# First shift and scale of an adaLN block: float32 weights straight to TensorE, in 32-column tiles of the array

## The chip, the cores and the metric

The kernel runs as one program on one NeuronCore of a Trainium2 chip. The metric is the device time of one execution in microseconds, and the median of three executions of the kernel before is 2047.05 us (2043.01 to 2047.86). The profile is of one further execution. PE is TensorE, DVE is VectorE, ACT is ScalarE, POOL is GpSimd and SP is SyncE, which issues the loads of the weights.

## The reference

One layer of a backbone is applied to 128 context tokens and 128 latent tokens, in float32, with a model width D of 2048. All of it lies behind a modulation that is computed from two conditioning vectors, `c_ctx` for the context tokens and `c` for the latent ones:

```python
mod = silu(c) @ w_mod + b_mod                       # w_mod is 2048 x 12288
shift1, scale1, gate1, shift2, scale2, gate2 = split(mod, 6)
h  = rmsnorm(x, norm1_g) * (1 + scale1) + shift1
...                                                 # w_in, three mixer branches, merge
x  = x + gate1 * (merged @ w_out)
h2 = rmsnorm(x, norm2_g) * (1 + scale2) + shift2
x  = x + gate2 * (square(relu(h2 @ w_ff1)) @ w_ff2)
```

So `w_mod` has six parts of 2048 x 2048. Of each part, two rows are wanted: one for each conditioning vector.

## The kernel before

**Units.** All weights come in units of 128 x 1024 float32 (512 KB). `run_stream` (L390) walks one list of steps for the whole layer. A step that holds a unit is prefetched: SP loads it into one of eight raw buffers (L399), and `split` (L384) turns it into two float32r tiles, a rounded one on ACT (`wh`) and the rest on DVE (`wl`). There are five buffers for such pairs (L400). PE multiplies each pair in three products per tile: high by high, low by high, high by low. This is the code of almost every group on the page, and it all carries line 171, that of the helper which records each call, so that groups are told apart by the names of the tiles.

**The first two parts of `w_mod`** (shift1 and scale1) are 64 units, `in_wmods`, in eight blocks of 256 columns. They go through the same split. For each k-tile, `do` (L656) multiplies the 128 x 512 high tile by a stationary tile of four columns (the high and low parts of silu(c) and silu(c_ctx)), and the 128 x 512 low tile by its first two columns. The result is a 4 x 512 row block in PSUM. After a block, `chain` (L678) copies the block out, turns it by four small matmuls with the constant `sel`, adds the bias, and makes the 256 rows of the modulated, normalised input `Hh`, `Hl` that go with these columns. The first 24 units of the input projection `w_in` (`in_win`, `in_winh`) stand between the 64 units, one after every two or three of them, from the 14th on.

**The other four parts** (gate1, shift2, scale2, gate2) take another way: `mods` (L732) is a background generator. It loads `in_wmodr` units by SP into three buffers `mraw`, and DVE multiplies each unit by a broadcast vector `cb` and sums it: two instructions per unit, one for each vector, into `junk` and `part`. That is 128 units and 256 such instructions. Each part has two halves of 16 units. Between halves the one `cb` buffer is loaded anew by POOL, and an add moves `part` into `modc`.

**What sets their order.** Nothing but the planner in the kernel does: `pump` (L302) lets generators go on while its model of the clock says that DVE and ACT are not behind PE. `mods` also waits for a quota (L757): unit m may be taken once `self.units`, which counts the steps that `run_stream` has done (L445), has reached `quota(m)` (L723). The quota is drawn through five marks (L1440, L1532, L1708), which are counts of all units in the list of steps. At three places the rest is forced, whatever the quota says. Part 2 is wanted by the output projection. Parts 3 and 4 are wanted ahead of the last piece of the output projection, in `drain_mod` (L1593, L1805), since the second norm needs them. Part 5 is wanted in `gates2` (L1679), which stands between the two halves of the third group of the second MLP matrix; there `chunk_rows` (L1733) turns the vector by a PE transpose and sends it to memory.

Of the kernel before, what the change touches and what calls it, by code (L numbers as in the profile page):

```python
# [7 lines left out]
F32 = mybir.dt.float32  # L8
# [6 lines left out]
P = 128  # L15
# [101 lines left out]
class Meter:  # L117
# [5 lines left out]
    def cost(self, name, a, k, out):  # L123
        n = int(np.prod(out.shape[1:]))
        src = k.get("in0", k.get("in_", a[1] if len(a) > 1 else out))
        ps = getattr(src, "space", None) == bass.MemoryType.PSUM
        if self.key == "pe":
            if name == "transpose":
                return max(n * 8.5e-4, 0.107)
            return n * 4.17e-4 + 0.0133 if k["rhs"].dtype == F32R else max(n * 1.7e-3, 0.22)  # L130
        if self.key == "act":
            fn = a[2] if len(a) > 2 else None
            extra = 0.0
            if fn in TABLES and self.clock.table != fn:
                self.clock.table, extra = fn, 1.3
            extra += 0.093 * sum(isinstance(k.get(x), bass.AP) for x in ("scale", "bias", "accum_out"))
            return (0.053 if ps else 0.095) + n * 8.3e-4 + extra
        if self.key == "pool":
            return 0.1 + n * 1.0e-3
        if name == "tensor_reduce":  # L140
            n = int(np.prod(src.shape[1:]))
        one = name in ("tensor_scalar", "tensor_copy", "memset") and not ps
        c = 0.07 + n * (6.3e-3 if name == "reciprocal" else 5.2e-4 if one else 1.04e-3)
        if isinstance(k.get("scalar", k.get("scalar1")), bass.AP):
            c += 0.06
        if "accum_out" in k:
            c += 0.116
        return c
# [46 lines left out]
class Backbone:  # L195
# [194 lines left out]
    def run_stream(self, steps):  # L390


        nc = self.nc
        units = [s["unit"] for s in steps if "unit" in s]
        raw, hl = [], {}
        st = dict(dma=0, front=0)
        t = self.t

        raws = [None] * 3 + [3, 4, 5, 6, 7]  # L399
        pairs = [None] * 3 + [8, 9]  # L400

        def issue():
            while raws and st["dma"] < len(units):
                n = st["dma"]
                z = raws.pop(0)
                u = units[n]
                if z is None:
                    w = self.rawp.tile([P, NB], F32, tag="raw", name=self.nm("raw"))[:, :u.shape[1]]
                else:
                    w = self.slot(z, [P, NB])  # L410
                nc.sync.dma_start(w, u)
                raw.append((w, self.clock.dma + DMA1, z))
                st["dma"] += 1

        def front():
            n = st["front"]
            s = steps[n]
            st["front"] += 1
            if "unit" not in s:
                return  # L420
            w, at, z = raw.pop(0)
            c = w.shape[1]
            p = pairs.pop(0)
            if p is None:
                hi = self.hlp.tile([P, NB], F32R, tag="wh", name=self.nm("wh"))[:, :c]
                lo = self.hlp.tile([P, NB], F32R, tag="wl", name=self.nm("wl"))[:, :c]
            else:
                both = self.slot(p, [P, 2, NB], F32R)
                hi, lo = both[:, 0, :], both[:, 1, :]
            self.split(hi, lo, w)  # L430
            hl[n] = (hi, lo, p, max(t["act"], t["dve"]) + READY)
            if z is None or st["dma"] < self.lend - 8:
                raws.append(z)
            issue()

        issue()
        for i, s in enumerate(steps):
            while st["front"] < len(steps) and pairs and not ("hold" in s and st["front"] > i):
                if st["front"] > i and raw and raw[0][1] > t["pe"] + 1.5:
                    break  # L440
                front()
            if s["kind"] == "mm":
                hi, lo, p, _ = hl.pop(i)
                s["do"](hi, lo)
                self.units += 1  # L445
                self.next = min((v[3] for v in hl.values()), default=0.0)
                self.pump()
                self.next = 0.0
                if p is None or st["dma"] < self.lend:
                    pairs.append(p)  # L450
            elif s["kind"] == "call":
                s["do"]()
# [49 lines left out]
    def setup(self):  # L502
        nc, I = self.nc, self.I
        c = lambda name, shape, dt=F32: self.cp.tile(shape, dt, tag=name, name=name)
        self.xin = [self.slot(10, [P, 8, 256]), self.slot(11, [P, 8, 256])]
        j, cv = self.take()
        cv = cv[:, :32]
        nc.sync.dma_start(cv, I["cvec"])
        for i in range(2):
            nc.sync.dma_start(self.xin[i], I["xT"][:, 8 * i:8 * i + 8, :])  # L510
        self.modc = c("modc", [P, 6, 16, 2])
        self.gs = c("gs", [P, 2, 16, 2])
        self.sel = c("sel", [4, 2])
        nc.scalar_dma.dma_start(self.sel, I["sel"])

        self.cs = c("cs", [P, 16, 2])
        nc.scalar.activation(self.cs.rearrange("p k v -> p (k v)"), cv, AF.Silu)
        self.puttmp(j)
        self.cst = c("cst", [P, 16, 4], F32R)
        self.split(self.cst[:, :, 0:2], self.cst[:, :, 2:4], self.cs)  # L520
        self.par = c("par", [P, 386])
        nc.scalar_dma.dma_start(self.par, I["par"])
        self.ident = c("ident", [P, P])
        nc.scalar_dma.dma_start(self.ident, I["ident"])
        self.tri = c("tri", [P, 4, P])
        self.hmask = c("hmask", [P, 7, P], U8)
        self.rows = c("rows", [P, 32])
        par = self.par
        self.bmod = par[:, 0:96].rearrange("p (c n) -> p c n", c=6)
        self.n1g, self.n2g = par[:, 96:112], par[:, 112:128]  # L530
        self.hlb = par[:, 128:144]
        self.hgn, self.gdnn = par[:, 144:145], par[:, 145:146]
        self.vng = par[:, 146:154]
        self.conv = par[:, 154:370].rearrange("p (n w) -> p n w", n=24)
        self.ones = c("ones", [P, P])
        nc.vector.memset(self.ones, 1.0)
        self.lb = c("lb", [P, 16])
        self.junk = c("junk", [P, 1024], mybir.dt.bfloat16)
        self.junk2 = c("junk2", [P, 512], mybir.dt.bfloat16)
        self.oml = c("oml", [P, 16])  # L540
# [82 lines left out]
    def start_steps(self, first, second):  # L623
# [32 lines left out]
        def do(db, u, hi, lo):  # L656
            if u == 0:
                if db >= 2:
                    self.finish(self.chains[db - 2])
                st[db] = self.grab()  # L660
            if (db, u) == (4, 0):
                self.hm = self.mid(2, [P, 7, P])
                nc.gpsimd.dma_start(self.hm, self.I["hmask"])
                nc.gpsimd.dma_start(self.tri, self.I["tri"])
                nc.gpsimd.dma_start(self.rows, self.I["rows"].partition_broadcast(P))
            if (db, u) == (6, 0):
                self.add(bounds())
                self.spread()
            o = st[db][1]
            for j in range(2):  # L670
                k = 2 * u + j
                w = slice(512 * j, 512 * j + 512)
                nc.tensor.matmul(o[:4], lhsT=self.cst[:, k, :], rhs=hi[:, w], start=(k == 0), stop=False, skip_group_check=True)
                nc.tensor.matmul(o[:2], lhsT=self.cst[:, k, 0:2], rhs=lo[:, w], start=False, stop=(k == 15), skip_group_check=True)
            if u == 7:
                self.chains[db] = self.add(chain(db), first=True)

        def chain(db):  # L678
            i, b = st[db]
            row = self.mid(db % 2, [P, 512])  # L680
            nc.scalar.copy(row[:4], b[:4])
            yield W
            for t in range(4):
                nc.tensor.matmul(b[:, 2 * t:2 * t + 2], lhsT=row[:4, t * P:t * P + P], rhs=self.sel, start=True, stop=True)
            yield W
            n0 = 2 * db
            nc.vector.tensor_tensor(out=self.modc[:, 0:2, n0:n0 + 2, :],
# [4 lines left out]
            while "r" not in st:  # L692
# [1 line left out]
            yield from self.modulate(0, n0, self.xin[n0 // 8][:, n0 % 8:n0 % 8 + 2, :], st["r"])  # L694

        steps = []
        mods = [[dict(kind="mm", unit=self.I["wmods"][db, u], do=lambda hi, lo, db=db, u=u: do(db, u, hi, lo))
                 for u in range(8)] for db in range(8)]
        wins = []
        for db in range(8):  # L700
# [1127 lines left out]
def layout(x_prompt, x_sample, c, state_hgrn, state_gdn, c_ctx, norm1_g, norm2_g, w_mod, b_mod, w_in,  # L1828
# [21 lines left out]
        m = 1 << j  # L1850
        hm[:, j] = (i[:, None] // (2 * m) == i[None] // (2 * m)) & (i[:, None] // m != i[None] // m)
    A["hmask"] = hm
    A["sel"] = np.tile(np.eye(2, dtype=f), (2, 1))
    A["rows"] = np.concatenate([gdn_A_log[0].reshape(-1), gdn_dt_bias[0].reshape(-1)])
    A["bs"] = cm_bs[0].reshape(-1)
    A["wsT"] = cm_ws[0].transpose(2, 0, 1)
# [43 lines left out]
```

## Time and profile before

| | |
|---|---|
| median of three executions | 2047.05 us |
| the profiled execution: its time | 2050.43 us |
| its span | 2048.7 us |
| bytes read from memory | 447.97 MB |
| the split, on DVE | x610 in the largest group, 741.6 us, 1221 ns each |
| the split, on ACT | x610 in the largest group, 637.1 us, 1048 ns each |
| DVE products of `mods` | x256, 312.2 us, 1219 ns each |

The page gives the busy time of each engine, the span in 40 slices of about 51 us, the chain of work that ended last, and the costliest groups of instructions. The ends of matmuls are modelled, so the start of one to the start of the next is the better measure of their pace. Other views list instructions in order of time, the waits of one engine, and busy times by stretch.

### The profile page before, as it was taken

To read this page: it belongs to the slowest core of one execution; us is meant where nothing else is said; L and a number is where in the kernel's file an instruction comes from. 1 tells how busy PE (TensorE), PEld (TensorE's weight loads), DVE (VectorE), ACT (ScalarE), POOL (GpSimd) and SP (SyncE) were. 2 spreads that over 40 slices of the span, in tenths; PEclk is the share of its full clock that TensorE was granted. 3 is DMA by queue.
4 is the path that set the end of the run, shared out by engine and by line. 5 is a ranking of instruction groups with operands and counts; after the bars stand their busy time and mean duration, and the time that the engine had idled before them with its cause. 6 is when DMAs were issued, how large, how long until landed. Compare 5 with 4: busy or idle time off the path is not lost.

```text
span 2048.7 us, 31030 instructions
## 1 busy us (share of the span) xinstructions
PE 1958.6 (96%) x12023; PEld 1727.4 (84%) x12023; DVE 1484.5 (72%) x2128; ACT 1013.3 (49%) x1486; POOL 49.1 (2%) x120
## 2 busy tenths in 40 slices
PE   5999999999999999999999997699999999999997
PEld 3769988999888889888888876599988998998886
DVE  6875797978887998556876878766676676555475
ACT  6774645476645544366434433444444443344343
POOL 0000000000000000110000000000000000000000
PEclk9999999999999999999999998799999999999998
DMA  9876665655567757655687777466667667566663
GB/s 339 312 288 216 206 206 195 217 192 184 178 206 232 261 195 246 216 185 194 232 301 252 256 279 253 158 202 222 225 228 254 217 227 237 191 201 210 208 235 136
DMA packets 124508, 460.55 MB, mean 225 GB/s; under 512 B 14216, under 2 KB 14792, under 8 KB 122184
## 3 DMA queue, kind: packets, MB, share of 16 engines
q1 hardware_dynamic: 116496, 423.96, 61.0%
q0 software_dynamic: 7568, 34.35, 4.9%
q8 instruction: 94, 1.54, 0.3%
q14 instruction: 54, 0.44, 0.1%
q10 hardware_dynamic: 296, 0.26, 0.0%
HBM read 447.97 MB, written 10.53 MB: 224 GB/s over the span
## 4 chain that ended last, share of the span: by engine, by line
PE 56%; DVE 9%; DMA 4%; ACT 2%; issue 2%; POOL 0%; DVEq 0%; ACTq 0%; SPq 0%; POOLq 0%
PE pb L171 53%; PE pf L171 4%; DVE wl L171 3%; DVE z L171 2%; DVE junk L171 1%; DVE m L171 1%; ACT wh L171 1%; DMA raw<-in_win 1%; DMA z<-in_s0gd 1%; DMA raw<-in_wouta 1%; DMA raw<-in_woutb 1%; DMA raw<-in_woutc 0%; DVE pf L171 0%; DMA mraw<-in_wmodr 0%; ACT L171 0%
## 5 line engine op out<-in xcount | busy, mean ns | idle before, releaser
L171 DVE TENSOR_TENSOR wl<-raw,wh 128x1024 fp32r<-128x1024 f32 x610 | 741.6, 1221 | 471.6 <-ACT wh L171 470.9
L171 ACT CAST wh<-raw 128x1024 fp32r<-128x1024 f32 x610 | 637.1, 1048 | 828.4 <-PE pb L171 686.3
L171 PE MATMUL pb<-Hh,wh 128*128 128x256 f32 x1864 | 533.4, 286 | 5.5 <-ACT Hh L171 3.1
L171 PE MATMUL pb<-Hl,wh 128*128 128x256 f32 x1864 | 529.8, 284 | 1.1 <-DVE Hl L171 1.1
L171 PE MATMUL pb<-Hh,wl 128*128 128x256 f32 x1864 | 529.6, 284 | 0.2 <-DVE wl L171 0.2
L171 PE MATMUL pb<-wh,z 128*128 128x512 f32 (+1 forms) x1472 | 444.2, 383 | 3.3 <-ACT z L171 3.3
L171 PEld LDWEIGHTS pb<-Hh,wh 128*128 128x128 f32 x1864 | 358.6, 192 | 8.1 <-ACT Hh L171 3.3
L171 PEld LDWEIGHTS pb<-Hl,wh 128*128 128x128 f32 x1864 | 358.4, 192 | 1.6 <-DVE Hl L171 1.5
L171 PEld LDWEIGHTS pb<-Hh,wl 128*128 128x128 f32 x1864 | 358.7, 192 | 1.1 <-DVE wl L171 0.4
L171 PE MATMUL pb<-wh,Hh 128*128 128x512 f32 (+1 forms) x800 | 317.0, 396 | 24.8 <-ACT wh L171 22.8
L171 PEld LDWEIGHTS pb<-wh,z 128*128 128x128 f32 x1472 | 273.2, 189 | 59.5 <-ACT z L171 4.5
L171 DVE SCALAR_TENSOR_TENSOR junk<-mraw,cb 128x1024 bf16<-128x1024 f32 x256 | 312.2, 1219 | 4.7 <-DMA mraw<-in_wmodr 2.4
L171 PE MATMUL pb<-wl,Hh 128*128 128x512 f32 (+1 forms) x800 | 307.0, 384 | 3.4 <-DVE wl L171 3.4
L171 PE MATMUL pb<-wh,Hl 128*128 128x512 f32 (+1 forms) x800 | 306.4, 383 | 0.0
L171 PE MATMUL pb<-wl,z 128*128 128x512 f32 (+1 forms) x736 | 281.8, 383 | 0.9 <-DVE wl L171 0.9
L171 PEld LDWEIGHTS pb<-wh,Hh 128*128 128x128 f32 x800 | 151.9, 190 | 53.5 <-ACT wh L171 23.7
L171 PEld LDWEIGHTS pb<-wl,Hh 128*128 128x128 f32 x800 | 151.9, 190 | 30.6 <-DVE wl L171 5.3
L171 PEld LDWEIGHTS pb<-wh,Hl 128*128 128x128 f32 x800 | 151.5, 189 | 29.7
L171 PEld LDWEIGHTS pb<-wl,z 128*128 128x128 f32 x736 | 138.5, 188 | 28.8 <-DVE wl L171 1.1
L171 DVE TENSOR_TENSOR z<-z,z 128x512 f32<-128x512 f32 (+4 forms) x120 | 90.8, 788 | 13.2 <-ACT z L171 9.4
L171 DVE SCALAR_TENSOR_TENSOR cy<-z,par,cy 128x258 f32<-128x258 f32 (+1 forms) x192 | 53.7, 332 | 1.9
L171 PEld LDWEIGHTS pf<-m,z 128*128 128x128 f32 x384 | 49.7, 191 | 3.7 <-ACT z L171 0.4
(187 smaller groups left out, 1366.0 us busy)
## 6 DMA issues: line engine op xcount, KB each, us to landing
raw<-in_win SPq DMA_DIRECT2D x249, 512.0 KB, 4.0
raw<-in_wff SPq DMA_DIRECT2D x224, 512.0 KB, 4.3
mraw<-in_wmodr SPq DMA_DIRECT2D x128, 512.0 KB, 5.4
raw<-in_wbr SPq DMA_DIRECT2D x48, 512.0 KB, 4.2
z<-in_wmods SPq DMA_DIRECT2D x39, 512.0 KB, 5.6
raw<-in_wmods SPq DMA_DIRECT2D x25, 512.0 KB, 6.3
cb<-csd POOLq DMA_DIRECT2D x8, 1024.0 KB, 7.7
raw<-in_wouta SPq DMA_DIRECT2D x16, 512.0 KB, 4.5
```

What stands on the lines that cost most here:

```text
L171: return f(*a, **k)
```

## The change

The 64 units of shift1 and scale1 are no longer split. The stationary tile is now plain float32 and 32 columns wide (two with the conditioning vectors, 30 of zeros), and the raw 128 x 512 float32 tile is the moving operand of one matmul for each k-tile. K-tile k writes 32 rows of PSUM from row 32 * (k % 3) on, with `tile_position=(0, 32 * (k % 3))`, so three k-tiles in a row belong to three different 32-column tiles of the array. The row block in PSUM is 96 x 512 in place of 4 x 512, and `sel` adds the three groups up when the block is turned. In `run_stream` such a step is marked `whole`: it needs no pair of split buffers, its raw buffer is given back after its matmuls, and it leaves the loop by `continue`.

```diff
+            if "tile_position" in k:
+                return n * 8.4e-4
...
+            if "whole" in s:
+                hl[n] = (w, None, z, at)
+                return
...
-            while st["front"] < len(steps) and pairs and not ("hold" in s and st["front"] > i):
-                if st["front"] > i and raw and raw[0][1] > t["pe"] + 1.5:
+            while st["front"] < len(steps) and (pairs or "whole" in steps[st["front"]]) and not ("hold" in s and st["front"] > i):
+                if st["front"] > i and (raw and raw[0][1] > t["pe"] + 1.5 or len(hl) > 4) or not raw and "unit" in steps[st["front"]]:
                     break
...
                 s["do"](hi, lo)
+                if "whole" in s:
+                    if p is None or st["dma"] < self.lend - 8:
+                        raws.append(p)
+                    issue()
+                    self.pump()
+                    continue
                 self.units += 1
...
-        self.cst = c("cst", [P, 16, 4], F32R)
-        self.split(self.cst[:, :, 0:2], self.cst[:, :, 2:4], self.cs)
+        self.cst = self.sp.tile([P, 8, 2, P], F32, tag="cb", name="cst").rearrange("p a b c -> p (a b c)")[:, :512].rearrange("p (k v) -> p k v", k=16)
+        nc.vector.memset(self.cst, 0.0)
+        nc.vector.tensor_copy(self.cst[:, :, 0:2], self.cs)
...
-                nc.tensor.matmul(o[:4], lhsT=self.cst[:, k, :], rhs=hi[:, w], start=(k == 0), stop=False, skip_group_check=True)
-                nc.tensor.matmul(o[:2], lhsT=self.cst[:, k, 0:2], rhs=lo[:, w], start=False, stop=(k == 15), skip_group_check=True)
+                g = 32 * (k % 3)
+                nc.tensor.matmul(o[g:g + 32], lhsT=self.cst[:, k, :], rhs=hi[:, w], start=(k < 3), stop=(k > 12),
+                                 skip_group_check=True, tile_position=(0, g))
...
-            nc.scalar.copy(row[:4], b[:4])
+            nc.scalar.copy(row[:96], b[:96])
...
-                nc.tensor.matmul(b[:, 2 * t:2 * t + 2], lhsT=row[:4, t * P:t * P + P], rhs=self.sel, start=True, stop=True)
+                nc.tensor.matmul(b[:, 2 * t:2 * t + 2], lhsT=row[:96, t * P:t * P + P], rhs=self.sel[:96], start=True, stop=True)
...
-    A["sel"] = np.tile(np.eye(2, dtype=f), (2, 1))
+    A["sel"] = np.tile(np.eye(32, dtype=f)[:, :2], (4, 1))
```

Three places show how the instructions stand. The first is PE at the start of the program, before: `pf_155` is the PSUM tile of the first block, `wh` and `wl` are split units, `cst` is the stationary tile.

```order
L171 MATMUL pf_155<-wh_149,cst 4x512
L171 MATMUL pf_155<-wl_150,cst 2x512
L171 MATMUL pf_155<-wh_149,cst 4x512
L171 MATMUL pf_155<-wl_150,cst 2x512
L171 MATMUL pf_162<-ones,m_4_111 128x1 x2
L171 MATMUL pf_162<-ones,tp_160 128x1 x4
```

The same place on PE in the changed kernel, where `raw_133`, `raw_135`, `raw_137` and `z_14_139` are units as they were loaded:

```order
L173 MATMUL pf_149<-raw_133,cst 32x512 x2
L173 MATMUL pf_149<-raw_135,cst 32x512 x2
L173 MATMUL pf_160<-ones,m_4_111 128x1 x2
L173 MATMUL pf_160<-ones,tp_158 128x1 x4
L173 MATMUL pf_149<-raw_137,cst 32x512 x2
L173 MATMUL pf_149<-z_14_139,cst 32x512 x2
```

A unit has two matmuls in place of four, and no split stands ahead of them on ACT or DVE.

The second place is DVE ahead of the last piece of the output projection, where `drain_mod` forces parts 3 and 4. Before, with the last two splits ahead of it and the add and `gs` that end it:

```order
L171 TENSOR_TENSOR wl_11427<-raw_11330,wh_11426 128x1024
L171 SCALAR_TENSOR_TENSOR junk,part_10925<-mraw_11222,cb_10923 128x1024
L171 TENSOR_TENSOR wl_11458<-raw_11367,wh_11457 128x1024
L171 SCALAR_TENSOR_TENSOR junk,part_10925<-mraw_11301,cb_10923 128x1024 x2
L171 SCALAR_TENSOR_TENSOR junk,part_10925<-mraw_11423,cb_10923 128x1024 x2
L171 SCALAR_TENSOR_TENSOR junk,part_10925<-mraw_11463,cb_10923 128x1024 x2
L171 SCALAR_TENSOR_TENSOR junk,part_10925<-mraw_11467,cb_10923 128x1024 x2
L171 SCALAR_TENSOR_TENSOR junk,part_10925<-mraw_11471,cb_10923 128x1024 x2
L171 SCALAR_TENSOR_TENSOR junk,part_10925<-mraw_11475,cb_10923 128x1024 x2
L171 SCALAR_TENSOR_TENSOR junk,part_10925<-mraw_11479,cb_10923 128x1024 x2
L171 SCALAR_TENSOR_TENSOR junk,part_10925<-mraw_11483,cb_10923 128x1024 x2
L171 SCALAR_TENSOR_TENSOR junk,part_10925<-mraw_11487,cb_10923 128x1024 x2
```

Then follow the add into `modc` and `gs`. In the changed kernel the last split there is `wl_11015`. Behind it stand 13 rows of this kind (26 instructions) on `cb_10654`, the add that ends the first half of part 4, 16 rows (32 instructions) on a new `cb_11073`, the add and `gs`, with nothing else between them. These rows are the seam between the halves:

```order
L173 SCALAR_TENSOR_TENSOR junk,part_10656<-mraw_11052,cb_10654 128x1024 x2
L173 SCALAR_TENSOR_TENSOR junk,part_10656<-mraw_11056,cb_10654 128x1024 x2
L173 SCALAR_TENSOR_TENSOR junk,part_10656<-mraw_11060,cb_10654 128x1024 x2
L173 TENSOR_TENSOR modc<-part_10656,par 128x32
L173 SCALAR_TENSOR_TENSOR junk,part_11075<-mraw_11064,cb_11073 128x1024 x2
L173 SCALAR_TENSOR_TENSOR junk,part_11075<-mraw_11068,cb_11073 128x1024 x2
```

So 58 products stand in one row where 18 stood, and a reload of `cb` stands among them.

The third place is DVE at `gates2`, at the end of a half of the second MLP matrix: four adds take the accumulators out of PSUM, and splits follow. Before:

```order
L171 TENSOR_TENSOR z_2114_14151<-pb_17133,z_2114_14151 128x512
L171 TENSOR_TENSOR z_2114_14151<-pb_17134,z_2114_14151 128x512
L171 TENSOR_TENSOR wl_17430<-raw_17375,wh_17429 128x1024
L171 TENSOR_TENSOR wl_17458<-raw_17393,wh_17457 128x1024
L171 TENSOR_TENSOR wl_17476<-raw_17411,wh_17475 128x1024
```

In the changed kernel:

```order
L173 TENSOR_TENSOR z_1996_13732<-pb_16742,z_1996_13732 128x512
L173 TENSOR_TENSOR z_1996_13732<-pb_16743,z_1996_13732 128x512
L173 TENSOR_TENSOR wl_17055<-raw_16996,wh_17054 128x1024
L173 SCALAR_TENSOR_TENSOR junk,part_15512<-mraw_16934,cb_15510 128x1024 x2
L173 SCALAR_TENSOR_TENSOR junk,part_15512<-mraw_17010,cb_15510 128x1024 x2
L173 SCALAR_TENSOR_TENSOR junk,part_15512<-mraw_17060,cb_15510 128x1024 x2
L173 TENSOR_TENSOR modc<-part_15512,modc 128x32
L173 TENSOR_TENSOR wl_17099<-raw_17017,wh_17098 128x1024
```

The last six products of part 5 and its add now stand here. On PE of the changed kernel the transpose of `chunk_rows`, which needs that add, stands between the last matmul of the one half and the first matmul of the next; before, it stood in the middle of an earlier block.

More of the change, by code (lines that the diff above doesn't have):

```diff
@@ L512, in setup @@
         self.gs = c("gs", [P, 2, 16, 2])
-        self.sel = c("sel", [4, 2])
+        self.sel = c("sel", [P, 2])
         nc.scalar_dma.dma_start(self.sel, I["sel"])
@@ L696, in start_steps @@
         steps = []
-        mods = [[dict(kind="mm", unit=self.I["wmods"][db, u], do=lambda hi, lo, db=db, u=u: do(db, u, hi, lo))
+        mods = [[dict(kind="mm", unit=self.I["wmods"][db, u], whole=True, do=lambda hi, lo, db=db, u=u: do(db, u, hi, lo))
                  for u in range(8)] for db in range(8)]
```

## The prediction

> **What bounds the kernel now.** I read the page first: busy times, then the slices.
>
> ```profile
> PE 1958.6 (96%) x12023; PEld 1727.4 (84%) x12023; DVE 1484.5 (72%) x2128; ACT 1013.3 (49%) x1486; POOL 49.1 (2%) x120
> ...
> PE   5999999999999999999999997699999999999997
> ```
>
> PE is the bound but for two places: the first slice, and the two slices near 1230 to 1330 us. So a change pays where PE idles, or by taking matmuls from PE. The busy times by stretch (stretch, its length, PE, PEld, DVE, ACT, POOL, clock, DMA share, GB/s) say how much there is to win or lose.
>
> ```profile
> 0.00:158.00 158.00, 134.57 (x786) 92.25 (x786) 114.51 (x133) 110.62 (x144) 3.03 (x9) 0.96 0.86 312
> ...
> 640.00:775.00 135.00, 129.57 (x707) 111.75 (x707) 123.39 (x241) 72.05 (x126) 5.43 (x10) 1.00 0.65 222
> ...
> 1260.00:1290.00 30.00, 7.12 (x56) 6.63 (x54) 25.56 (x44) 3.80 (x8) 0.00 (x0) 0.66 0.61 207
> ```
>
> The first 158 us hold the work that the change touches: PE idles 23.4 us there, and DMA is 86% busy. The stretch at 1260 us belongs to `drain_mod`: DVE works and PE does not. The instructions in order of time show it, DVE first, then PE.
>
> ```profile
> 1259.70 1.23 DVE L171 TENSOR_TENSOR wl<-raw,wh 128x1024 fp32r<-128x1024 f32 x1 [0.30 <-ACT wh L171]
> 1260.85 1.22 DVE L171 SCALAR_TENSOR_TENSOR junk<-mraw,cb 128x1024 bf16<-128x1024 f32 x1
> ...
> 1268.05 1.22 DVE L171 SCALAR_TENSOR_TENSOR junk<-mraw,cb 128x1024 bf16<-128x1024 f32 x1 [2.18 <-DMA mraw<-in_wmodr]
> ...
> 1284.52 1.22 DVE L171 SCALAR_TENSOR_TENSOR junk<-mraw,cb 128x1024 bf16<-128x1024 f32 x1
> ```
> ```profile
> 1266.26 0.28 PE L171 MATMUL pb<-wh,Hl 128*128 128x256 f32 x1
> 1289.38 0.58 PE L171 MATMUL pb<-wh,Hh 128*128 128x256 f32 x1 [22.84 <-ACT wh L171]
> ```
> ```profile
> 1287.03 0.42 ACT L171 ACTIVATE junk<-z 128x256 bf16<-128x256 f32 x1 [25.84 <-DVE z L171]
> ```
>
> A train of 18 products runs from 1260.85 to past 1284.52, and PE, with nothing split ahead, waits 22.84 us. The wait is put down to ACT, but ACT itself stood 25.84 us behind DVE, with a square that needs DVE's result and has the casts behind it.
>
> **Part 1: the quota falls behind, and the train grows.** This is the term that decides. The new branch leaves the loop by `continue`, ahead of `self.units += 1`, while the marks still count the 64 units. So all quotas come 64 steps late, the background products move to later places, and what the drain forces grows: the order has 58 products in one row where it had 18. From 1268.05 to 1284.52 are 13 intervals, 1.267 us each. So 40 more products take 40 x 1.267 = 50.7 us. Loads of `mraw` keep up: in the train of before there is one wait for them, at its start. But the longer train spans the seam of part 4, where `cb` is loaded anew.
>
> ```profile
> 1189.88 0.19 DVE L171 TENSOR_TENSOR modc<-part,par 128x32 f32<-128x32 f32 x1
> ...
> 1190.14 0.53 POOL L171 DMA_DIRECT2D cb<-csd  x1 [148.75 <-DVE modc L171]
> ...
> 1197.50 1.23 DVE L171 SCALAR_TENSOR_TENSOR junk<-mraw,cb 128x1024 bf16<-128x1024 f32 x1 [0.93 <-DMA cb<-csd]
> ```
>
> From the add to the next product are 7.6 us, with splits in between to fill them; in the train nothing fills them. I take 7.5. Behind DVE's train wait the splits, behind them PE, and no PE work covers it: the 5.4 us between 1260.85 and 1266.26 are used up already. Sum: **+58 us**, between 48 (DVE, with less before it, reaches the train 10 us earlier) and 66 (four waits for `mraw` like the 2.18).
>
> **Part 2: the same at `gates2`.** Six products, 6 x 1.267 = 7.6 us, the add and the transpose of `chunk_rows` now stand between two halves of the second MLP matrix.
>
> ```profile
> 1901.09 2.48 DVE L171 TENSOR_TENSOR z<-pb,z 128x512 f32<-128x512 f32 x4
> 1903.49 1.22 DVE L171 TENSOR_TENSOR wl<-raw,wh 128x1024 fp32r<-128x1024 f32 x1
> ```
> ```profile
> 1757.39 0.19 DVE L171 TENSOR_TENSOR modc<-part,modc 128x32 f32<-128x32 f32 x1
> 1757.62 0.25 ACT L171 COPY tp<-modc 128x32 f32<-128x32 f32 x1 [2.66 <-DVE modc L171]
> ...
> 1758.46 0.27 PE L171 MATMUL pf<-ident,tp 128*32 128x128 f32 x1
> ```
>
> PE ends the half about 0.5 us ahead of the last add, which ends at 1903.57; one split takes 1.1 us more, the products 7.6, and from the add to the transpose are 1.1 us. So PE, which today goes straight on there, stands some 10 us. The stretch of the long wait has a granted clock of 0.66, so PE resumes slowly; my estimate for that is 2 us more. **+12 us**, between 6 and 15. In what lies between, products only change places: PE idles 5.4 us in the densest stretch, 640 to 775. I cost that at nothing; the cover is PE's own work, and 5 us either way is the price if it fails.
>
> **Part 3: the matmuls of shift1 and scale1.** Four matmuls a unit are removed, 256 in all, and two a unit added, 128.
>
> ```profile
> L171 PE MATMUL pf<-wl,cst x78: 387/392/628, 17.0 to 157.8; 128*2 128x512 f32 x78
> ...
> 34.50 0.40 PE L171 MATMUL pf<-wl,cst 128*2 128x512 f32 x1
> 34.73 0.40 PE L171 MATMUL pf<-wh,cst 128*4 128x512 f32 x1
> ```
> ```profile
> 18.20 0.84 PE L171 MATMUL pf<-ones,m 128*128 128x1 f32 x4
> ...
> 806.13 1.05 PE L171 MATMUL pf<-m,z 128*128 128x128 f32 x8
> 807.02 1.06 PE L171 MATMUL pf<-m,m 128*128 128x128 f32 x8
> ```
>
> Removed: 256 x 0.23 = 59 us of PE, the last of them at 157.8 us. A float32 matmul is two records: the order has two instructions `pf<-ones,m`, the trace four. Eight records with 128 columns take 0.89 us, 0.111 each, so one with 512 columns takes 0.445 and a matmul 0.89. Alone, 128 of them take 114 us; if three tiles run fully side by side, 38 us. Neither is in this trace. PE starts matmuls in order, and the second record of a matmul must follow its first on the same tile, so I expect that only the second record of one and the first of the next overlap: one slot of 0.445 per matmul, and one more for each run of such units. There are 20 runs (14 units, then twos and threes between units of `w_in`), so 148 x 0.445 = 66 us: +7 against 59. This is nearest to the row of 0.111 with what the order allows; the ends stay in the range.
>
> The Trainium skill, "TensorE: Matmul & The Clock Gate", section "Measured speedup vs the span model", gives 2.38 times for three column tiles with 512 columns. By it the 128 would take 114 / 2.38 = 48 us and the forecast would be 18 us lower, close to rival (b) below; no run here shows it yet.
>
> What switching to tiles and back costs is not in the trace. 40 switches at nothing, or at the 0.16 us by which a matmul's 0.39 us outlasts its pace of 0.23, are 0 to 6 us; I take 3. The Trainium skill, "TensorEngine Tiling (Array Packing)", section "Key Properties", says that a change of mode drains TensorE, which speaks against this change, without a price.
>
> On the other side the first units of `w_in` may start earlier.
>
> ```profile
> 42.74 0.58 PE L171 MATMUL pb<-Hl,z 128*128 128x256 f32 x1 [2.31 <-DVE Hl L171]
> ...
> 20.00:30.00 10.00, 9.05 (x31) 3.52 (x32) 9.11 (x13) 5.54 (x8) 0.00 (x0) 1.00 1.00 361
> ```
>
> Today PE waits until 42.74 for the first `Hl`, behind splits on DVE. The removed splits (64 x 1.22 = 78 us of DVE) clear that path. Then the loads bind: 15 units of 0.524 MB and 2.1 MB of `x` at 361 GB/s from 2 us on are landed near 30, and with the cast PE starts near 33, 9 us earlier at most. Later a raw buffer is held until PE is done with it, which makes the prefetch shallower. I take 5 of the 9. Part 3 in sum: 7 + 3 - 5 = **+5 us**.
>
> **Sum.** 58 + 12 + 5 = 75 us over the profiled execution's 2050.4 (its span 2048.7 and 1.7 around it) is 2125. The median of the runs is 3.4 us below that execution, so the forecast is **2122 us**.
>
> **Rivals.** (a) *No tiles side by side.* 128 x 0.89 is 114 us, 55 more than today. The first 28 matmuls hide 12 of these (28 x (0.89 - 0.46)) under the first loads, and with PE still busy on them the earlier start is lost: part 3 is 55 - 12 + 3 = 46, and the time 2122 + 41 = 2163. For it: each matmul has two records that must follow each other. (b) *Three tiles fully side by side.* PE loses 21 us, but 88 units at 1.45 us and the first loads bind near 137 us, and today's last such matmul is at 157.8 with its chain behind; I take part 3 as -16, so 2101. (c) *The freed DVE pays it all back*: not slower. Suppose every microsecond of DVE freed ahead of the train shortens the time: 40 products are 50.7 us, and the PE idle of the first 158 us another 23.4, together 74, so 2048. It decides from about 69 us on. For it, 123.39 of 135 us of DVE at 640; against it, PE is busy 129.57 there, so there are 5 us to win, not 50.
>
> **How the numbers follow.** The forecast has 0.62, with its own range 2108 to 2136 (part 1 from 48 to 66, part 2 from 6 to 15); (a) 0.20, (b) 0.13, (c) 0.05. A measurement of this kernel can tell about 0.3% from no change, 6 us, so from 2041 to 2053 is the same. (c) lies on that line: 0.03 same and 0.02 faster; all else is slower, 0.95. The range, 2096 to 2166, takes in (a) and (b).
>
> **What would show it.** DVE near 1260 us must have 58 products in one train with one gap of about 7 us, and PE one wait of about 80 us. PE must wait some 10 us for a transpose near 1970. The starts of records with `cst` tell the tiles: 0.445 us from one matmul to the next is mine, 0.89 is (a), 0.30 is (b). If the train is there but PE waits far less than 80 us, part 1 is wrong; if PE's last `cst` matmul ends more than 15 us away from today's 158, part 3 is.

## The result, and the profile after

The changed kernel takes 2102.82 us in the median of four executions (2095.32 to 2106.37), beside 2046.92 us for the kernel before on the same chip. The ratio is 1.0272, with a 95% interval of 1.0241 to 1.0303: slower by 2.7%, 56 us. The profiled spans are 2048.7 us before and 2100.2 us after, 51.5 us apart.

The page of the changed kernel, first its busy times and then PE in 40 slices:

```profile
PE 1943.7 (93%) x12023; PEld 1713.6 (82%) x12023; DVE 1416.7 (67%) x2065; ACT 951.3 (45%) x1419; POOL 48.9 (2%) x120
...
PE   6989999999999999999999960599999999999897
```

PE is busy 15 us less than before and DVE 68 us less, and yet the span is longer. One hole has grown: in slices 24 to 26 PE stands at 6, 0 and 5 tenths. The busy times by stretch put it into one place (stretch, its length, PE, PEld, DVE, ACT, POOL, clock, DMA share, GB/s):

```profile
0.00:158.00 158.00, 131.28 (x842) 87.70 (x843) 48.26 (x77) 57.35 (x89) 3.03 (x9) 0.96 0.89 329
...
640.00:775.00 135.00, 130.72 (x765) 116.16 (x764) 126.87 (x241) 65.70 (x109) 9.33 (x21) 0.99 0.70 238
...
1250.00:1350.00 100.00, 15.14 (x86) 14.02 (x86) 78.02 (x142) 11.51 (x27) 2.12 (x4) 0.54 0.60 197
```

From 1250 to 1350 us PE works for 15 of 100 us. DVE's instructions in order of time there (start, duration, and in brackets the idle time before and what ended it):

```profile
1236.53 1.23 DVE L173 TENSOR_TENSOR wl<-raw,wh 128x1024 fp32r<-128x1024 f32 x1
...
1237.67 1.22 DVE L173 SCALAR_TENSOR_TENSOR junk<-mraw,cb 128x1024 bf16<-128x1024 f32 x1
...
1245.10 1.23 DVE L173 SCALAR_TENSOR_TENSOR junk<-mraw,cb 128x1024 bf16<-128x1024 f32 x1 [2.40 <-DMA mraw<-in_wmodr]
...
1272.98 0.19 DVE L173 TENSOR_TENSOR modc<-part,par 128x32 f32<-128x32 f32 x1
...
1283.38 1.23 DVE L173 SCALAR_TENSOR_TENSOR junk<-mraw,cb 128x1024 bf16<-128x1024 f32 x1 [10.21 <-DMA cb<-csd]
...
1322.66 1.22 DVE L173 SCALAR_TENSOR_TENSOR junk<-mraw,cb 128x1024 bf16<-128x1024 f32 x1
```

And PE beside it, two rows that follow one another:

```profile
1243.71 0.28 PE L173 MATMUL pb<-wh,Hl 128*128 128x256 f32 x1
1327.51 0.58 PE L173 MATMUL pb<-wh,Hh 128*128 128x256 f32 x1 [83.53 <-ACT wh L173]
```

No split stands between 1237.67 and 1323.88. The train has one wait for `mraw` near its start, as before, and one for the reload of `cb`, 10.40 us from the add to the next product. PE waits 83.53 us where it waited 22.84.

The second place is `gates2`, DVE, ACT and PE in order of time:

```profile
1949.71 1.22 DVE L173 SCALAR_TENSOR_TENSOR junk<-mraw,cb 128x1024 bf16<-128x1024 f32 x1
...
1950.98 0.19 DVE L173 TENSOR_TENSOR modc<-part,modc 128x32 f32<-128x32 f32 x1
1951.21 0.25 ACT L173 COPY tp<-modc 128x32 f32<-128x32 f32 x1 [10.03 <-DVE modc L173]
...
1951.51 0.40 PE L173 MATMUL pf<-ident,tp 128*32 128x128 f32 x1 [11.41 <-ACT tp L173]
```

PE waits 11.41 us for the transpose there.

To see where else the time went, the same matmul is found in both traces: the n-th one into `pb`, which both kernels issue in the same order. Its start after, less its start before:

| start before, us | 115 | 156 | 183 | 506 | 734 | 805 | 1006 | 1249 | 1289 | 1871 | 1906 | 2035 |
|---|---|---|---|---|---|---|---|---|---|---|---|---|
| after minus before, us | -11.9 | -18.7 | -10.2 | -9.4 | -19.7 | -5.9 | -20.6 | -21.3 | +38.1 | +38.5 | +52.0 | +52.1 |

So the changed kernel is 10.2 us ahead after the stage that the change is about, 21.3 ahead at the train, loses 59.5 there and 13.5 at `gates2`. The 13.5 are 2 us more than the wait of 11.41: from 1951.5 to 1956 us the granted clock was 0.56, so PE resumed slowly, for which the prediction had set 2 us.

The matmuls of the change themselves, PE in order of time, from a run of six (units in `raw` and `z` buffers):

```profile
51.46 0.28 PE L173 MATMUL pb<-Hl,wh 128*128 128x256 f32 x1
51.67 0.62 PE L173 MATMUL pf<-z,cst 128*32 128x512 f32 x2
51.68 0.62 PE L173 MATMUL pf<-raw,cst 128*32 128x512 f32 x1
52.12 0.60 PE L173 MATMUL pf<-z,cst 128*32 128x512 f32 x2
52.14 1.01 PE L173 MATMUL pf<-raw,cst 128*32 128x512 f32 x2
52.56 0.60 PE L173 MATMUL pf<-z,cst 128*32 128x512 f32 x2
52.98 0.59 PE L173 MATMUL pf<-raw,cst 128*32 128x512 f32 x1
52.99 0.60 PE L173 MATMUL pf<-z,cst 128*32 128x512 f32 x2
53.52 0.50 PE L173 MATMUL pb<-Hh,z 128*128 128x256 f32 x2
```

The counts add up to twelve records, which are six matmuls (the row of 1.01 us holds two records, one after the other). Three records start within 0.02 us of 51.67, three more 0.45 us later, and so on, four times in all: three k-tiles run beside each other, and six matmuls take from 51.67 to 53.52, 1.85 us or 0.31 each.

### The profile page after: what moved, and what is told of

Its sections match the earlier page's. It is cut to its first block, busy times and chain, and to the rows that moved or that the text cites. A ratio compares the mean times of both kernels' runs of the same rounds, so it can differ in the third digit from the quotient of the medians.

```text
span 2100.2 us, 30783 instructions
## 1 busy us (share of the span) xinstructions
PE 1943.7 (93%) x12023; PEld 1713.6 (82%) x12023; DVE 1416.7 (67%) x2065; ACT 951.3 (45%) x1419; POOL 48.9 (2%) x120
## 4 chain that ended last, share of the span: by engine, by line
PE 75%; DVE 10%; issue 6%; DMA 5%; ACT 3%; SPq 0%; POOL 0%; DVEq 0%; ACTq 0%; POOLq 0%
PE pb L173 67%; PE pf L173 7%; DVE wl L173 3%; DVE junk L173 2%; DVE z L173 2%; ACT wh L173 1%; DVE m L173 1%; DMA z<-in_win 1%; DMA raw<-in_win 1%; DMA cb<-csd 1%; ACT z L173 1%; DMA raw<-in_winh 1%; DMA z<-in_xT 0%; DMA z<-in_s0gd 0%; ACT tp L173 0%
## 5 line engine op out<-in xcount | busy, mean ns | idle before, releaser
L173 DVE TENSOR_TENSOR wl<-raw,wh 128x1024 fp32r<-128x1024 f32 x594 | 723.0, 1220 | 541.2 <-ACT wh L173 540.0
L173 ACT CAST wh<-raw 128x1024 fp32r<-128x1024 f32 x594 | 621.5, 1048 | 822.8 <-PE pb L173 695.4
L173 DVE SCALAR_TENSOR_TENSOR junk<-mraw,cb 128x1024 bf16<-128x1024 f32 x256 | 312.2, 1220 | 15.8 <-DMA cb<-csd 10.2
L173 PEld LDWEIGHTS pb<-wl,z 128*128 128x128 f32 x736 | 138.9, 189 | 29.1 <-DVE wl L173 1.3
L173 DVE TENSOR_TENSOR z<-z,z 128x512 f32<-128x512 f32 (+4 forms) x104 | 71.7, 721 | 17.3 <-ACT z L173 13.5
L173 ACT ACTIVATE junk<-z 128x512 bf16<-128x512 f32 (+1 forms) x20 | 10.9, 544 | 112.2 <-DVE z L173 112.2
```

The costliest lines, as they stand in the source:

```text
L173: return f(*a, **k)
```

## The experiments

My theory after the result: the quota's lag makes the train and the wait at `gates2`, as the prediction said, and without it the change would be a small gain. The rivals: the lag is not the cause, and the mode of the matmuls or the raw buffers, held longer, cost the time; or the start's gain is worth more than it shows. What made the start faster was open too: the tiles of the array, or the splits that DVE and ACT no longer do.

**1. Count the 64 steps.** The changed kernel, with the count that `continue` passes by put back.

```diff
                     issue()
+                    self.units += 1
                     self.pump()
                     continue
```

> The changed kernel with one line more: a whole step counts in self.units again. Theory (the lag of the quota is the loss, the matmuls are a gain): the train ahead of the last piece of the output projection is 18 products long again and PE waits about 23 us there, the wait of 11.4 us at gates2 is gone, and the 10.5 us that the changed kernel is ahead at 200 us stay: 2047 - 10.5 = 2036 us. Of the 11 us that it gains between 570 and 1010 us, the theory says that they came from products moved to later places, so they go as well. Rival 1: these 11 us come from the removed splits and stay: 2025 us. Rival 2: the train is a matter of DVE being short of time and not of the count: 58 products stay and the time stays near 2100 us.

Measured: 2040.26 us, ratio 0.9965 (0.9953 to 0.9978). PE's waits, in the order of the kernel (waited for: us in total, times, longest):

```profile
PE pb L173 <- ACT wh L173: 24.8, 3, 22.4
```

The train has 18 products again, and the wait at `gates2` is not in the list. By the same comparison of matmuls this kernel is 8.8 us ahead at 183 us and as much at the end; by the medians it is 6.4, so the theory's 10.5 was 4 too many. One line was worth 62.6 us, and the rest of the change is a gain of 0.35%. The 11 us that the changed kernel won between 600 and 1250 us are gone as well.

**2. The lag alone.** The kernel before, with the same 64 steps not counted and all else left.

```diff
-                self.units += 1
+                self.units += "late" not in s
...
-        mods = [[dict(kind="mm", unit=self.I["wmods"][db, u], do=lambda hi, lo, db=db, u=u: do(db, u, hi, lo))
+        mods = [[dict(kind="mm", unit=self.I["wmods"][db, u], late=True, do=lambda hi, lo, db=db, u=u: do(db, u, hi, lo))
```

> The kernel before, all of it, with one change: the 64 steps of shift1 and scale1 are not counted in self.units. Theory: the lag alone gives the stalls that the changed kernel shows (59.5 us at the train, 13.5 at gates2) and the 11 us won between: 2047 + 62 = 2109 us. Rival: the stalls need the raw buffers that are held longer or the tiles: within 10 us of 2047 us.

Measured: 2110.47 us, ratio 1.0307 (1.0283 to 1.0331).

```profile
PE pb L171 <- ACT wh L171: 85.2, 2, 84.3
...
PE pf L171 <- ACT tp L171: 11.5, 1, 11.5
```

Both waits are there, without a single matmul changed. Against the kernel before, this one is level at 487 us, 10.9 us ahead at 1218, 49.1 behind at 1347 and 63.1 behind at 2009. So the lag gives all three: the 11 us won on the way, the train and `gates2`. That settles the slowdown.

**3. No tiles side by side.** Experiment 1 with all k-tiles in the first 32 columns; the row block is 32 x 512, and the start and end of the sum, the copy and `sel` follow from that (not shown).

```diff
-                g = 32 * (k % 3)
+                g = 0
...
```

> e1_counted with every k-tile in the same 32-column tile (rows 0 to 31 of PSUM, one accumulation of 16), nothing side by side. Theory: 0.85 us from one matmul to the next in place of 0.43, 128 x 0.42 = 54 us more of PE, of which about 12 hide under the first loads: e1_counted + 42, about 2078 us. Rival (nothing ran side by side, a 32-column matmul is just short): same as e1_counted within 3 us.

Measured: 2092.01 us, ratio 1.0230 (1.0208 to 1.0252). The same run of six matmuls on PE:

```profile
55.17 1.91 PE L173 MATMUL pf<-raw,cst 128*32 128x512 f32 x4
56.91 3.60 PE L173 MATMUL pf<-z,cst 128*32 128x512 f32 x8
60.44 0.39 PE L173 MATMUL pb<-Hh,wh 128*128 128x256 f32 x1
```

They take 5.27 us, 0.88 each, as worked out from the small matmuls before. The tiles are worth 52 us against experiment 1, ten more than expected: without them this kernel is 45 us slower than the one before, close to the 46 that rival (a) gave this stage.

**4. Two tiles.** Experiment 1 with `k % 2`, two column tiles in place of three; the row block is 64 x 512.

```diff
-                g = 32 * (k % 3)
+                g = 32 * (k % 2)
...
```

> e1_counted with two 32-column tiles in turn (k % 2) in place of three. Theory (only the second half of one matmul and the first half of the next overlap, so two tiles are enough): 0.43 us from one matmul to the next and the same time as e1_counted within 3 us. Rival (three run side by side): pace 0.43 becomes 0.6 or more, 10 to 25 us slower than e1_counted.

Measured: 2047.65 us, ratio 1.0017 (1.0003 to 1.0030). This is 7 us above experiment 1. My theory, that only neighbours overlap and so a third tile brings nothing, fell; the rival was right that three run side by side, but its price of 10 to 25 us was too high.

```profile
51.23 1.05 PE L173 MATMUL pf<-z,cst 128*32 128x512 f32 x4
52.12 1.03 PE L173 MATMUL pf<-raw,cst 128*32 128x512 f32 x4
52.97 1.03 PE L173 MATMUL pf<-z,cst 128*32 128x512 f32 x4
53.93 0.51 PE L173 MATMUL pb<-Hh,z 128*128 128x256 f32 x2
```

Six matmuls take 2.70 us here, 0.45 each, against 0.88 on one tile and 0.31 on three: n tiles run n side by side. What is at its limit then is seen by stretch. From 60 to 120 us, first the changed kernel, then two tiles:

```profile
60.00:120.00 60.00, 59.20 (x422) 40.76 (x422) 20.89 (x34) 24.38 (x38) 0.51 (x1) 1.00 0.96 357
```
```profile
60.00:120.00 60.00, 60.00 (x385) 38.99 (x384) 18.92 (x29) 22.32 (x35) 0.51 (x1) 1.00 0.91 332
```

With two tiles PE has no idle time, and a block takes 17.6 us from one copy of its row block to the next. With three a block takes 15.9 us:

```profile
74.91 0.58 ACT L173 COPY m<-pf 96x512 f32<-96x512 f32 x1 [2.45 <-PE pf L173]
90.80 0.58 ACT L173 COPY m<-pf 96x512 f32<-96x512 f32 x1 [2.84 <-PE pf L173]
106.66 0.58 ACT L173 COPY m<-pf 96x512 f32<-96x512 f32 x1 [2.12 <-PE pf L173]
```

A block has 11 units of 0.524 MB, which at the 361 GB/s of the loads at the start is 16.0 us. So with three tiles the loads are at their limit. PE is nearly full too, but by this estimate, which no run tests, a still faster matmul would bring little in this stretch.

**5. The splits as dead work.** Experiment 1, with the cast on ACT and the subtraction on DVE put back for each of the 64 units, into a spare buffer and `junk`. Nothing reads them.

```diff
             if "whole" in s:
+                h = self.rawp.tile([P, NB], F32, tag="mraw", name=self.nm("spare"))
+                nc.scalar.copy(h, w)
+                nc.vector.tensor_tensor(out=self.junk, in0=w, in1=h, op=ALU.subtract)
                 hl[n] = (w, None, z, at)
```

> e1_counted, with the split of the 64 units put back on ACT and DVE as work whose result nobody reads (a cast to a spare buffer, a subtraction into junk); the matmuls still take the raw units. Theory (the gain of the first 160 us comes from fewer microseconds on PE, and the loads bind there): the freed DVE and ACT are worth little, 2040 us, within 3 us of e1_counted. Rival (the freed DVE and ACT bring the first unit of w_in forward by 4.5 us and keep PE fed): most of the gain of 6 to 9 us goes, 2045 to 2049 us.

Measured: 2050.01 us, ratio 1.0012 (1.0003 to 1.0021). My theory, that the freed time of DVE and ACT is worth little, fell: this kernel is 10 us slower than experiment 1.

```profile
60.00:120.00 60.00, 57.31 (x380) 38.33 (x381) 48.53 (x53) 45.29 (x58) 0.00 (x0) 0.94 0.91 323
```

No engine is full: PE 57.31, DVE 48.53 and ACT 45.29 of 60 us, the loads at 0.91; the granted clock is 0.94 where it was 1.00 with three tiles and no splits. A block takes 17.2 to 18.4 us, no less than the 17.2 before the change. So with such work left on ACT and DVE the tiles brought nothing here. Which wait binds stays open; the spare buffer also takes turns with the loads of `mraw`, so not all of the 10 us need be the splits'.

**6. The quota drawn earlier.** Experiment 1, with parts 2 to 4 due sooner: 84 of their 96 units by the second mark, in place of 72. This tests from the other side that the forced train is what PE waits for.

```diff
-        if m < 72:
-            return a + (b - a) * m / 72
+        if m < 84:
+            return a + (b - a) * m / 84
         if m < 96:
-            return b + (c - b) * (m - 72) / 24
+            return b + (c - b) * (m - 84) / 12
```

> e1_counted with the quota drawn steeper: 84 units instead of 72 up to the second mark, 12 instead of 24 behind it, so that the train of 18 products ahead of the last piece of the output projection is gone from DVE's order. Theory (the train is the wait, product by product): PE's wait of 22.4 us there goes to under 3 us, and earlier products cost up to 5 us: 2040 - 18 = 2022 us. Rival (DVE is short of time before that place and gives it back in late splits): 2035 us or more.

Measured: 2009.43 us, ratio 0.9816 (0.9800 to 0.9832). There is no train, and the wait of 22.4 us is gone from PE's list. Between 1181 and 1347 us this kernel gains 28.9 us on the kernel before. The theory took the wait, less 5 us for earlier products, and gave 2022; the gain over experiment 1 is 31 us, not 18. Some 4 us beyond the wait lie right behind it: there PE starts its matmuls 0.21 us apart in experiment 1, at a granted clock of 0.50, and the same ones 0.12 us apart here, at 1.00. Another 4 were won ahead of 1249 us; these I did not trace.

**7. Raw buffers given back longer.** Experiment 1 was 8.8 us ahead at 183 us though PE's last `cst` matmul came 19 us earlier in the changed kernel, so something gives time back between. Where the planner's count of issued loads comes within eight of `self.lend`, one of the five numbered raw buffers (`z` in the trace) that has been used is no longer taken up again. The edit, at two places, moves that limit twelve loads further.

```diff
-            if z is None or st["dma"] < self.lend - 8:
+            if z is None or st["dma"] < self.lend + 4:
...
-                    if p is None or st["dma"] < self.lend - 8:
+                    if p is None or st["dma"] < self.lend + 4:
```

> e1_counted, in which the five raw buffers in the numbered slots go on being used for 12 loads more at the end of the first stage (lend + 4 in place of lend - 8, two places). Theory (between 125 and 155 us only three raw buffers are left, and a raw unit of shift1 and scale1 holds one until PE is done with it, so loads start late and PE waits): the 9 us lost between 137 and 172 us come back, 2040 - 8 = 2032 us. Rival (the loads themselves bind, 88 units at 1.45 us): no change, 2040 us within 2 us.

Measured: 2029.85 us, ratio 0.9911 (0.9898 to 0.9924). The stretch from 140 to 150 us, first experiment 1, then this kernel:

```profile
140.00:150.00 10.00, 2.92 (x16) 1.60 (x16) 2.70 (x3) 3.42 (x4) 0.56 (x1) 0.93 0.86 304
```
```profile
140.00:150.00 10.00, 9.24 (x75) 8.84 (x75) 5.53 (x8) 5.67 (x9) 0.56 (x1) 1.00 0.94 360
```

PE goes from 2.92 to 9.24 of 10 us and the loads from 304 to 360 GB/s. The loads that SP issues in experiment 1 show why:

```profile
130.11 6.11 SPq L173 DMA_DIRECT2D raw<-in_wmods  x2
136.32 0.37 SPq L173 DMA_DIRECT2D raw<-in_win  x1
139.92 0.33 SPq L173 DMA_DIRECT2D raw<-in_winh  x1
```

After 125 us only buffers named `raw` are loaded, where this kernel goes on with `z` too. The start is now worth 23.2 us at 183 us in place of 8.8, of which 19.2 are left from 1347 us on.

**8. Experiments 6 and 7 together.** Both edits on experiment 1.

> e6_quota_ahead and e7_buffers_longer in one. Theory: the two gains lie in different stages and add up: 2022 - 8 = 2014 us. Rival (the earlier end of the first stage makes DVE late at the train again): 2022 us or more.

Measured: 1995.16 us, ratio 0.9747 (0.9733 to 0.9761), faster than either kernel of this study. The expectation was too careful, since it took experiment 6 at less than it gave. The page of this kernel:

```profile
PE 1938.6 (97%) x12023; PEld 1710.0 (86%) x12023; DVE 1411.7 (71%) x2065; ACT 954.7 (48%) x1422; POOL 48.9 (2%) x120
...
PE   6999999999999999999999998999999999999997
```

**9. The same two edits without the change.** The kernel before with the quota of experiment 6 and the limit of experiment 7.

> The kernel before, with the two edits of e8_both (quota drawn steeper, numbered raw buffers used for 12 loads more) and nothing of the change. Theory: the train goes as in e6_quota_ahead, which won 31 us over e1_counted; the longer use of the raw buffers brings little, since a raw buffer is free here as soon as it is split (0 to 4 us): 2047 - 31 - 2 = 2014 us, so that 19 us of e8_both's gain are the change's own. Rival (the buffers are worth as much here as in e7_buffers_longer, 10 us or more): 2006 us or less. Rival 2 (with 78 us of splits more on DVE the steeper quota is not reached): 2025 us or more.

Measured: 2013.55 us, ratio 0.9847 (0.9830 to 0.9864). The total held, but its terms did not: at 183 us this kernel is 7.8 us ahead of the kernel before, where experiment 2, with the lag alone, is 1.3 ahead, so the buffers brought some 6 us here and not 2, against 14 at the same place in experiment 7. The change itself, with its count put right and both edits around it, is worth 18 us by the medians (1995.16 against 2013.55) and 20 by the ratios; the other 32 come from the two edits, which help the kernel before as well.

## Why the prediction was right, and where it was wrong

Forecast 2122 us, measured 2102.82; the sign was right, and so was the cause. The time lies 5 us below the forecast's own range of 2108 to 2136, and nearer to rival (b), which had a chance of 0.13. The medians stand 56 us apart and the profiled spans 51.5, so some 4 us are the spread of single executions. By the prediction's own terms, against the profiled spans:

| term | predicted, us | measured, us |
|---|---|---|
| part 1, the train | +58 | +59.5 |
| part 2, `gates2` | +12 | +13.5 |
| what lies between | 0, 5 either way | -11.1 |
| part 3, the stage of shift1 and scale1 | +5 | -10.2 |
| sum (measured at the matmul of 2035, with 0.4 between the rows) | +75 | +52.1 |

**Part 1 was right**, with its mechanism: one row of 58 products, one gap, one PE wait, and experiments 1 and 2 show that the missing count alone makes and unmakes it. The reload of `cb` cost 10.40 us in place of 7.5.

**Part 2 was right** in the same way, and experiment 2 shows the same wait of 11.5 us.

**What lies between was mis-sized.** The step "In what lies between, products only change places" took only the idle time of 640 to 775 us as a prize. Summed from 300 to 1249 us before, and over the same matmuls after, PE stands thus:

```profile
sum 949.00, PE 933.25 PEld 814.35 DVE 745.70 ACT 494.90 POOL 39.54; mean PE 133.32 PEld 116.34 DVE 106.53 ACT 70.70 POOL 5.65
```
```profile
sum 936.90, PE 928.22 PEld 812.35 DVE 720.27 ACT 492.15 POOL 37.59; mean PE 132.60 PEld 116.05 DVE 102.90 ACT 70.31 POOL 5.37
```

PE's idle time falls from 15.8 to 8.7 us, which is 7 of the 12 us. DVE has 25 us less to do on the way, since products come later; that this is what shortens PE's waits fits, but was not followed wait by wait. The remaining 5 are PE's busy time, and the cause of them stays open. The granted clock can explain about 1.6 of them: between 506 and 605 us it was 0.97 before and 1.00 after (3.3 us by estimate), between 734 and 804 it was 1.00 before and 0.98 after (1.7 the other way). Experiment 2, which changes the count alone, has 8.5 us of idle time over these matmuls, so it is the lag that wins them. The products put off are paid for again in the train, so experiment 1, which puts the count back, loses these 11 us too.

**Part 3 failed** at one step: "so I expect that only the second record of one and the first of the next overlap: one slot of 0.445 per matmul". Order within a tile does not hold up the other tiles. The six matmuls above took 1.85 us; by that step they would have taken seven slots, 3.1 us. That was rival (b)'s condition, and its price came close: -16 for the stage against -10.2, 2101 against 2102.82 for the whole. The prediction's own test, the end of the last `cst` matmul, said so as well:

```profile
L173 PE MATMUL pf<-raw,cst x104: 592/592/1061, 14.6 to 138.9; 128*32 128x512 f32 x104
```

It starts at 138.9 us where the last one of before started at 157.8, 19 us earlier. The loads were near their limit on the way, as (b) said (357 of 361 GB/s from 60 to 120 us), and part of the 19 us was given back to the raw buffers (experiment 7). That (b) hit the total is partly luck, since its sum has nothing for the 11 us on the way.

Of the page of the Trainium skill that was weighed, "TensorE: Matmul & The Clock Gate", section "Measured speedup vs the span model": it was on the right side, and the measurement decides the size. It gives 2.38 times for three column tiles with 512 columns; here 0.88 us on one tile became 0.31 on three, 2.8 times. Runs of four matmuls gained less, from 3.55 us to 1.83, 1.9 times: on three tiles four matmuls take two rounds, as six do.

Of the other terms of part 3, the 5 us for the earlier start held: the first matmul of `w_in` starts at 35.28 us where it started at 39.94. The 3 us for switching were too few. Into and out of a run the changed kernel shows

```profile
88.65 0.28 PE L173 MATMUL pb<-Hl,z 128*128 128x256 f32 x1
88.86 1.90 PE L173 MATMUL pf<-z,cst 128*32 128x512 f32 x8
90.69 0.39 PE L173 MATMUL pb<-Hh,wh 128*128 128x256 f32 x1
90.92 0.28 PE L173 MATMUL pb<-Hh,wl 128*128 128x256 f32 x1
```

and the kernel before

```profile
110.68 0.28 PE L171 MATMUL pb<-Hl,z 128*128 128x256 f32 x1
110.80 0.40 PE L171 MATMUL pf<-wh,cst 128*4 128x512 f32 x1
```

So the step into a run is 0.21 us in place of 0.12, the run takes 1.83 where two rounds of 0.89 us are 1.78, and the first step behind it is 0.23 in place of 0.12. That is 0.25 us a run, about 5 us in 20 runs, near the upper end of the 0 to 6. No run here tells whether the tiles or plain float32 cost it.

**Rival (a)** fell with the first rows of `cst`; experiment 3 shows that its price was right. **Rival (c)** fell too: of the 74 us that it needed, 21.3 were won ahead of the train.

## What to carry to other kernels

Where a new branch leaves a loop early, look for every counter behind it: here one skipped count, which no result depends on, pushed work to the places where it is forced and cost 63 us, where the rest of the change brought 6 to 7. A stage that gets a faster engine is worth only what its loads and its buffers let through, so after such a change read which of them now ends the wait, and look at the rules that stop prefetching at the stage's end. And forced work in a row, with nothing behind it to feed the bounding engine, is worth spreading even where it looks short: here the edit that took away 22 us of wait gave 31.

## What the runs showed of the hardware

Float32 matmuls of 32 columns with 512 columns to move took, in runs of six, 0.88 us each on one column tile, 0.45 on two and 0.31 on three, with float32r matmuls of the whole array directly before and behind them. The steps into and out of such a run were about 0.1 us longer each than between the matmuls around it. I had not expected the two records of one matmul to leave room for two other tiles. And a transfer may cost more in another place: the reload of `cb`, 7.6 us from the add to the next product where it stood before, took 10.40 us inside the train, and 10.69 inside that of experiment 2.
